# Two token streams that alternate by matmuls in place of weight units, in a four-layer float32 decoder trunk

## The chip, the core and the metric

The kernel runs on one core of one Trainium2 chip. A core has TensorE (matrix products, written into PSUM banks), ScalarE (ACT), VectorE (DVE), GpSimd (POOL) and SyncE (SP), whose queue starts the DMAs here. Each engine works through its own queue in order, and semaphores make one wait for another. The metric is the device time of one execution in microseconds. Three runs of the kernel before took 1221.28, 1221.42 and 1222.72 us; the median is 1221.42.

## What is computed

Four decoder layers over 256 tokens with a model width of 1024, all in float32. Each layer has a token mixer and a SwiGLU feed-forward part, each between two RMS norms. Layers 0 and 3 use differential attention with rotary positions, layer 1 stick-breaking attention, layer 2 sliding-window attention with sinks.

```python
for i in range(DEPTH):                     # 4 layers
    hn = rms_norm(x, norm_gains[i, 0])
    m = mixer(hn)                          # kind i % 3; input projection, attention, w_out
    x = x + rms_norm(m, norm_gains[i, 1])
    f = swiglu(rms_norm(x, norm_gains[i, 2]), ffn_w_gate[i], ffn_w_up[i], ffn_w_down[i])
    x = x + rms_norm(f, norm_gains[i, 3])

def swiglu(h, w_gate, w_up, w_down):       # hidden width 2816
    return (jax.nn.silu(h @ w_gate) * (h @ w_up)) @ w_down
```

(`mixer` stands here for the three attention functions.)

## The kernel before

**Tokens.** The 256 tokens are two streams of 128, stream 0 and stream 1. Both run through the same layers; stream 1 needs keys and values of stream 0.

**Weights.** All weights pass once through the core, cut into 378 units of 128 x 1024 float32 in the order in which a stream needs them. `load_dma` (L240) brings a unit into one of 4 staging buffers, `split` (L252) makes two float32r parts of it, `hi` on ScalarE and `lo` on VectorE, in a ring of 11 slots (L30, L162). A slot is free again when both streams have used its unit. Activations are split in the same way, and a product is the sum of three matmuls: high by hi, high by lo, low by hi.

**Products.** `project` (L494) does one chunk of an input projection, or of gate and up, into one PSUM bank: 4 units with six matmuls of 512 columns each (two blocks of 128 rows: hi, lo, hi, lo with the high part, and then two with the low part). In layer 2 a chunk has 2 units of twelve matmuls of 256 columns. `rows_product` (L468) adds one unit of an output or down projection to two banks, again in six matmuls; the two banks take turns except in the last unit, where one bank is finished before the other (`mm3`, L379). A feed-forward part has 11 chunks of 4 gate-and-up units; the two down units of a chunk follow one chunk later, so that a chunk in the middle costs a stream 6 units. After a chunk come the activation (`t`, `h`) and two transposes (`th`) that give the rows for the down projection.

**Order.** The program is unrolled, and `Emitter` (L41) sets the order in which instructions are emitted. Each stream is a generator that asks for the next unit (`("w",)`), asks to be resumed no earlier than a delay (`("d", ns)`, counted on an estimate of TensorE's time), or waits for an event (`("e", key)`). Attention pieces (transposes, scores, values) run as tasks beside the two streams. `run` (L123) looks at the tasks first in each round, then lets stream 0 go on if it can, otherwise stream 1. Stream 0 may be up to 8 units ahead (`LAG`, L33; `can`, L112). Where stream 1 has yet to pass an edge (the end of an input projection or of a layer) that stream 0 has passed, stream 1 comes first (L139, L140). Since a generator stops only to ask for a unit, a delay or an event, all six matmuls of a unit are emitted together: at full distance the streams alternate unit by unit. A scheduler below the emission assigns the buffers and the waits, and may move an instruction past others that are not ready.

**Small tiles.** Tiles of a few columns (sums, reciprocals, norms: `ss`, `u`, `r`, `nm`, `l`, `half` and others) are in the pool `wk` together with the large working tiles, some constants in `cst`.

All engine calls pass through `Start.run` (L179), so that nearly all rows of the profile name L180; they are told apart by the names of their tiles: `mm_f` gate and up, `acc_f` down, `mm_a`, `mm_b`, `mm_c` the input projections (`mm_a010q` is layer 0, stream 1, group 0, queries), `acc_a`, `acc_b`, `acc_c` the output projections, `th_f` the transposes of the hidden rows, `sc`, `tw`, `ta`, `tpr` and `pv` the attention pieces.

Of the kernel before, what the change touches and what calls it, by code (L numbers as in the profile page):

```python
# [9 lines left out]
F32 = mybir.dt.float32  # L10
# [8 lines left out]
P = 128  # L19
# [21 lines left out]
class Emitter:  # L41
    """Orders the emission of several generators by a running estimate of the tensor engine's time.

    A generator yields ("w",) for the next weight unit, ("d", ns) to be resumed no earlier than ns
    after the tensor engine's work emitted so far, or ("e", key) to wait for an event.
    """

    def __init__(self, load_dma, split, n_units, edges):
        self.t = 0.0
        self.load_dma, self.split, self.n, self.edges = load_dma, split, n_units, edges  # L50
        self.issued = self.loaded = 0
        self.pos = [0, 0]
        self.ring = {}
        self.events = set()
        self.limit = 0
        self.tasks = []
# [101 lines left out]
def trunk_kernel(ctx, tc, x, positions, norm_gains, a_w_in, a_w_out, a_lambda, a_subln, b_w_in, b_w_out,  # L158
# [5 lines left out]
    wk = ctx.enter_context(tc.tile_pool(name="wk", bufs=2))  # L164
    ps = ctx.enter_context(tc.tile_pool(name="ps", bufs=1, space=PSUM))
# [4 lines left out]
    class Start:  # L170
        """An engine whose instructions stay in the order of emission until the start is over."""
# [40 lines left out]
    def downs(c):  # L212
        """The chunks of the down projection that follow chunk c of the gate and up projections."""
# [55 lines left out]
    pos_i = cst.tile([P, 2], I32, name="pos_i")  # L269
# [10 lines left out]
    nsink = cst.tile([P, 16], F32, name="nsink")  # L280
# [4 lines left out]
    inv = cst.tile([P, 32], F32, name="inv")  # L285
    mhalf = cst.tile([P, 8], F32, name="mhalf")
    quarter = cst.tile([P, 1], F32, name="quarter")
    pool.memset(quarter, math.pi / 2)
    act.activation(wk.tile([P, 1], F32, tag="preload", name="preload", bufs=1), quarter, AF.Sin)
# [7 lines left out]
    # additive masks of a block of keys: causal, strictly causal, and the part of the window before the block  # L297
# [12 lines left out]
    gsub = cst.tile([P, 2], F32, name="gsub")  # L310
    lam_init = [0.8 - 0.6 * math.exp(-0.3 * i) for i in (0, 3)]
    nlam = cst.tile([P, 2], F32, name="nlam")
# [3 lines left out]
    def tables():  # L316
        """Generator: cos twice and sin with its sign, per position."""
        magic = 12582912.0
        posf = cst.tile([P, 2], F32, name="posf")
# [28 lines left out]
    def scalars():  # L348
        """-lambda, the negated sinks, and the gains of the inner norm."""
        lsum = wk.tile([P, 4], F32, tag="lsum", name="lsum", bufs=1)  # L350
# [28 lines left out]
    def mm3(o, ah, al, bh, bl, first, last):  # L379
        mm(o, ah, bh, first, False)  # L380
        mm(o, ah, bl, False, False)
        mm(o, al, bh, False, last)

# [4 lines left out]
    def rstd_of(name, s, ss, more=EPS, extra=None):  # L388
        """1/rms from the mean square, or from two parts of it."""
        u = wk.tile([P, 1], F32, tag=f"u{s}", name=f"u_{name}")  # L390
        r = wk.tile([P, 1], F32, tag=f"r{s}", name=f"r_{name}", bufs=3)
# [4 lines left out]
    def first_halves(s, tps, gs, th, tl, name):  # L396
        """The parts of the first layer's input, between the steps of the tables and the first weights."""
# [18 lines left out]
    def pre_norm(s, n, name):  # L416
        """x transposed, times the gain, in two parts; and 1/rms per token."""
        ss = wk.tile([P, 1], F32, tag=f"ss{s}", name=f"ss_{name}")
# [36 lines left out]
    def post_norm(s, acc, gain, name):  # L455
        ss = wk.tile([P, 2], F32, tag=f"ssp{s}", name=f"ssp_{name}")
# [64 lines left out]
    def scaled_tables(s, r, name):  # L521
        """The tables of the keys, and those of the queries, which carry the scores' scale."""
# [24 lines left out]
    def score_products(s, sc, q, k, mask):  # L547
        """The scores of two pairs of heads: the heads of even and of odd number, in half of the array's rows and a bank each."""
# [13 lines left out]
    def split_rows(oT, sl, src, scale=None):  # L562
        """src, times scale, as two float32r parts."""
# [8 lines left out]
    def layer_a(s, i, xn):  # L572
# [20 lines left out]
        def scores(g):  # L593
# [5 lines left out]
            l = st[g] = wk.tile([P, 2, 4], F32, tag=f"l{s}", name=f"l_{name}{g}", bufs=2)  # L599
            el = st[g, "el"] = wk.tile([P, 4], F32, tag=f"el{s}", name=f"el_{name}{g}", bufs=2)  # L600
            ws = {}
            for step in range(3):
                if step < 2:
# [5 lines left out]
                    nm = wk.tile([P, 2, 2], F32, tag=f"nm{s}", name=f"nm_{name}{g}{h0}")  # L609
# [9 lines left out]
                    r = wk.tile([P, 2], F32, tag=f"rl{s}", name=f"rl_{name}{g}{h0}")  # L619
# [19 lines left out]
        def values(g):  # L639
# [8 lines left out]
            ss = wk.tile([P, 4], F32, tag=f"os{s}", name=f"os_{name}{g}")  # L648
# [124 lines left out]
    def layer_c(s, i, xn):  # L773
# [19 lines left out]
        def heads(chunk, g):  # L793
# [17 lines left out]
            nm = wk.tile([P, 2, 2], F32, tag=f"nm{s}", name=f"nm_{name}{g}")  # L811
            es = wk.tile([P, 2, 2], F32, tag=f"es{s}", name=f"es_{name}{g}")
            l = wk.tile([P, 2, 2], F32, tag=f"l{s}", name=f"l_{name}{g}")
# [43 lines left out]
    def ffn(s, i, xn):  # L857
        name = f"f{i}{s}"
        half = wk.tile([P, 1], F32, tag=f"half{s}", name=f"half_{name}", bufs=1)
        hsq = wk.tile([P, 1], F32, tag=f"hsq{s}", name=f"hsq_{name}", bufs=1)  # L860
# [5 lines left out]
        def down(c):  # L866
            nonlocal acc
            for j in range(2):
# [4 lines left out]
                rows_product(acc, hT[c][0][:, j2, :], hT[c][1][:, j2, :], w, c == 0 and j == 0, c == NCH - 1 and j == 1)  # L873
# [78 lines left out]
```

## Time and profile before

| what | value |
|---|---|
| median of 3 runs | 1221.42 us |
| span of the profiled execution | 1220.4 us |
| instructions | 16738 |
| matmuls in the trace | 6028 |
| read from HBM | 203.76 MB, 168 GB/s over the span |
| DMA q1 (all weights) | 54.5% of 16 engines' span |

The profile shows one execution. In a row of groups, the two numbers after the bar are the busy time in all and the mean of one instruction; behind the second bar stands the idle time of the engine ahead of them and what ended it. PE is TensorE's matmuls, PEld its weight loads. In the chain that ended last, a piece has its start, its duration and the number of instructions merged in it, and a piece's duration counts each matmul from its start to the next one's. In the timeline a row has start, duration, engine, operation, output<-inputs and shape; rows that follow each other directly are merged, with their count. A wait's row has the waiting engine and tile, what it waited for, the sum in us, the number of waits and the longest.

### The profile page before, as it was taken

Reading aid. Unit: us, or ns where it says so; the run is one execution under the profiler, and the core shown is the slowest. Engines: PE = TensorE matmul, PEld = TensorE weight load, DVE = VectorE, ACT = ScalarE, POOL = GpSimd, SP = SyncE. Lnnn points to the kernel's source line nnn. Section 1 sums busy time; section 2 is a strip of 40 time slices with the busy share of each in tenths; the row PEclk is TensorE's granted clock in tenths of the full one; section 3 lists DMA queues with packets and bytes.
Section 4 is the critical chain, followed back from the end, with each engine's and each line's share of the span. In section 5 each row is a group of like instructions: output and inputs, shape, how many; then the busy total and the mean of one; then the engine's idle time right before and its main releaser. Section 6 shows DMA issues by size and latency. Waiting matters only on the chain.

```text
span 1220.4 us, 16738 instructions
## 1 busy us (share of the span) xinstructions
PE 1202.2 (99%) x6028; PEld 971.7 (80%) x6028; DVE 779.3 (64%) x1217; ACT 656.7 (54%) x1197; POOL 48.1 (4%) x141
## 2 busy tenths in 40 slices
PE   8999999999999999999999999999999999999997
PEld 6787788888878788888888778888878778888886
DVE  7866665555847666555578666555586776655553
ACT  5665644444756654444477664444474565544442
POOL 2000100000200000000000010000010001000000
PEclk9999999999999999999999999999999999999999
DMA  8635465566743546656564246565565453656550
GB/s 274 205 118 157 155 190 184 179 189 183 219 133 121 173 139 189 190 175 187 184 197 137 87 149 187 183 188 182 182 202 151 131 173 121 181 183 189 179 166 35
DMA packets 140838, 205.90 MB, mean 169 GB/s; under 512 B 9554, under 2 KB 104916, under 8 KB 140756
## 3 DMA queue, kind: packets, MB, share of 16 engines
q1 hardware_dynamic: 140048, 204.51, 54.5%
q8 instruction: 47, 0.77, 0.3%
q10 hardware_dynamic: 708, 0.34, 0.1%
q14 instruction: 35, 0.29, 0.1%
HBM read 203.76 MB, written 1.05 MB: 168 GB/s over the span
## 4 chain that ended last, share of the span: by engine, by line
PE 90%; DVE 4%; ACT 2%; issue 1%; DMA 1%; POOL 1%; DVEq 0%; ACTq 0%; POOLq 0%
PE mm_f L180 39%; PE acc_f L180 18%; PE acc_a L180 3%; PE mm_c L180 2%; PE acc_b L180 2%; DVE lo L180 2%; PE sc_a L180 2%; PE th_f L180 2%; PE acc_c L180 1%; PE sc_b L180 1%; ACT hi L180 1%; DMA stage<-in_a_w_in_dram 1%; PE pv_a L180 1%; PE sc_c L180 1%; DVE x L180 1%
## 5 line engine op out<-in xcount | busy, mean ns | idle before, releaser
L180 DVE TENSOR_TENSOR lo<-stage,hi 128x1024 fp32r<-128x1024 f32 x378 | 460.9, 1223 | 297.7 <-ACT hi L180 295.9
L180 ACT ACTIVATE hi<-stage 128x1024 fp32r<-128x1024 f32 x378 | 399.4, 1061 | 333.8 <-PE mm_f L180 160.0
L180 PE MATMUL mm_f<-hi,xh_q 128*128 128x512 f32 x704 | 283.5, 403 | 0.0
L180 PE MATMUL mm_f<-lo,xh_q 128*128 128x512 f32 x704 | 278.6, 396 | 0.0
L180 PE MATMUL mm_f<-hi,xl_q 128*128 128x512 f32 x704 | 221.0, 395 | 0.9 <-DVE xl_q L180 0.9
L180 PEld LDWEIGHTS mm_f<-hi,xl_q 128*128 128x128 f32 x704 | 132.5, 188 | 34.2 <-DVE xl_q L180 1.8
L180 PEld LDWEIGHTS mm_f<-hi,xh_q 128*128 128x128 f32 x704 | 132.3, 188 | 28.7 <-ACT xh_q L180 0.2
L180 PEld LDWEIGHTS mm_f<-lo,xh_q 128*128 128x128 f32 x704 | 132.4, 188 | 28.4
L180 PE MATMUL acc_f<-hi,hTh_f 128*128 128x512 f32 x352 | 114.9, 402 | 0.5 <-ACT hTh_f L180 0.5
L180 PE MATMUL acc_f<-hi,hTl_f 128*128 128x512 f32 x352 | 111.9, 394 | 0.8 <-DVE hTl_f L180 0.8
L180 PE MATMUL acc_f<-lo,hTh_f 128*128 128x512 f32 x352 | 111.5, 392 | 0.0
L180 ACT ACTIVATE t_f<-mm_f,half_f 128x256 f32<-128x256 f32 x88 | 41.8, 475 | 83.6 <-PE mm_f L180 82.6
L180 PEld LDWEIGHTS acc_f<-hi,hTl_f 128*128 128x128 f32 x352 | 65.9, 188 | 16.0 <-DVE hTl_f L180 1.4
L180 PEld LDWEIGHTS acc_f<-lo,hTh_f 128*128 128x128 f32 x352 | 66.1, 188 | 15.3
L180 PEld LDWEIGHTS acc_f<-hi,hTh_f 128*128 128x128 f32 x352 | 63.8, 188 | 13.4 <-ACT hTh_f L180 0.8
L180 DVE SCALAR_TENSOR_TENSOR t_f<-t_f,mm_f 128x256 f32<-128x256 f32 x88 | 36.7, 417 | 37.5 <-ACT t_f L180 37.4
L180 DVE SCALAR_TENSOR_TENSOR h_f<-t_f,hsq_f,mm_f 128x256 f32<-128x256 f32 x88 | 42.2, 480 | 2.7
L180 ACT ACTIVATE hTh_f<-th_f 128x256 fp32r<-128x256 f32 x88 | 33.0, 376 | 18.1 <-PE th_f L180 17.8
L180 DVE TENSOR_TENSOR hTl_f<-th_f,hTh_f 128x256 fp32r<-128x256 f32 x88 | 36.5, 418 | 5.9 <-ACT hTh_f L180 5.9
L180 ACT ACTIVATE e_a<-sc_a,nm_a 128x128 f32<-128x128 f32 (+1 forms) x64 | 26.0, 421 | 17.0 <-DVE nm_a L180 16.9
L180 PEld LDWEIGHTS th_f<-ident,h_f 128*128 128x128 f32 x176 | 24.4, 140 | 11.5
L180 PE MATMUL th_f<-ident,h_f 128*128 128x128 f32 x176 | 33.5, 272 | 0.0
(584 smaller groups left out, 1545.0 us busy)
## 6 DMA issues: line engine op xcount, KB each, us to landing
stage<-in_ffn_w_gate_dram SPq DMA_DIRECT2D x176, 256.0 KB, 2.8
stage<-in_ffn_w_up_dram SPq DMA_DIRECT2D x176, 256.0 KB, 3.1
stage<-in_ffn_w_down_dram SPq DMA_DIRECT2D x88, 512.0 KB, 3.5
stage<-in_a_w_in_dram SPq DMA_DIRECT2D x48, 512.0 KB, 3.9
stage<-in_b_w_in_dram SPq DMA_DIRECT2D x24, 512.0 KB, 3.8
stage<-in_a_w_out_dram SPq DMA_DIRECT2D x16, 512.0 KB, 3.7
stage<-in_c_w_in_dram SPq DMA_DIRECT2D x10, 512.0 KB, 3.8
gain<-in_norm_gains_dram SPq DMA_DIRECT2D x8, 512.0 KB, 4.1
```

The lines of the kernel that those rows point to most:

```text
L180: i = call(*args, **kw)
```

## The change

The generators of the products stop after each matmul with a new request, `("m",)`, which gives the turn to the other stream. The turn counts only while stream 0 is at least 7 units ahead; there the two streams now alternate matmul by matmul. Elsewhere the order of the streams is as before, but a round, with its look at the tasks and at the ring, now follows each matmul.

```diff
@@ class Emitter
+        self.turn = 0
...
@@ run_main
         elif what[0] == "e":
             m["want"] = what[1]
+        elif what[0] == "m":
+            self.turn = 1 - s
         else:
             m["want"] = "w"
...
@@ run
             behind = any(self.pos[1] < w <= self.pos[0] for w in self.edges)
-            order = mains[::-1] if behind else mains
+            apart = self.pos[0] - self.pos[1] >= LAG - 1
+            order = mains[::-1] if behind or apart and self.turn else mains
...
@@ rows_product
         cols = [slice(h * 512, (h + 1) * 512) for h in range(2)]
+        steps = [(h, a, v) for a, v in ((ah, 0), (ah, 1), (al, 0)) for h in range(2)]
         if last:
-            for h, cs in enumerate(cols):
-                mm3(acc[h], ah, al, w[0][:, cs], w[1][:, cs], first, last)
-        else:
-            for v in range(2):
-                for h, cs in enumerate(cols):
-                    mm(acc[h], ah, w[v][:, cs], first and v == 0, False)
-            for h, cs in enumerate(cols):
-                mm(acc[h], al, w[0][:, cs], False, False)
+            steps.sort(key=lambda step: step[0])
+        for h, a, v in steps:
+            mm(acc[h], a, w[v][:, cols[h]], first and v == 0 and a is ah, last and a is al)
+            yield ("m",)
...
@@ out_proj, and in the same way down in ffn
-            rows_product(acc, oh, ol, w, kt == 0, kt == KT - 1)
+            yield from rows_product(acc, oh, ol, w, kt == 0, kt == KT - 1)
...
@@ project
                 for v in range(2):
                     mm(b, xn[0][:, kt, :], w[v][:, cs], kt == 0 and v == 0, False)
+                    yield ("m",)
             for kt, cs in js:
                 mm(b, xn[1][:, kt, :], w[0][:, cs], False, kt == KT - 1)
+                yield ("m",)
...
@@ trunk_kernel
     wk = ctx.enter_context(tc.tile_pool(name="wk", bufs=2))
+    sm = ctx.enter_context(tc.tile_pool(name="sm", bufs=2))
```

The order of the matmuls within a unit stays. The small tiles, and the small constants of `cst`, are now taken from the pool `sm`, each with the number of buffers that it had, for example:

```diff
-        u = wk.tile([P, 1], F32, tag=f"u{s}", name=f"u_{name}")
+        u = sm.tile([P, 1], F32, tag=f"u{s}", name=f"u_{name}")
...
-    nsink = cst.tile([P, 16], F32, name="nsink")
+    nsink = sm.tile([P, 16], F32, name="nsink", bufs=1)
```

Docstrings and comments are gone, and with them nothing that runs.

More of the change, by code (lines that the diff above doesn't have):

```diff
@@ L267, in trunk_kernel @@
         nc.tensor.matmul(warm, zero, zero, start=True, stop=True)
-    pos_i = cst.tile([P, 2], I32, name="pos_i")
+    pos_i = sm.tile([P, 2], I32, name="pos_i", bufs=1)
     nc.scalar.dma_start(pos_i, positions.rearrange("b (s p) -> p (b s)", p=P))
@@ L283, in trunk_kernel @@
     nc.scalar.dma_start(nsink, c_sinks[0].partition_broadcast(P))
-    inv = cst.tile([P, 32], F32, name="inv")
-    mhalf = cst.tile([P, 8], F32, name="mhalf")
-    quarter = cst.tile([P, 1], F32, name="quarter")
+    inv = sm.tile([P, 32], F32, name="inv", bufs=1)
+    mhalf = sm.tile([P, 8], F32, name="mhalf", bufs=1)
+    quarter = sm.tile([P, 1], F32, name="quarter", bufs=1)
     pool.memset(quarter, math.pi / 2)
-    act.activation(wk.tile([P, 1], F32, tag="preload", name="preload", bufs=1), quarter, AF.Sin)
+    act.activation(sm.tile([P, 1], F32, tag="preload", name="preload", bufs=1), quarter, AF.Sin)
     for j in range(32):
@@ L309, in trunk_kernel @@
     gains = cst.tile([P, P], F32, name="gains")
-    gsub = cst.tile([P, 2], F32, name="gsub")
+    gsub = sm.tile([P, 2], F32, name="gsub", bufs=1)
     lam_init = [0.8 - 0.6 * math.exp(-0.3 * i) for i in (0, 3)]
-    nlam = cst.tile([P, 2], F32, name="nlam")
+    nlam = sm.tile([P, 2], F32, name="nlam", bufs=1)
     cosf = cst.tile([P, 2, 64], F32, name="cosf")
@@ L318, in tables @@
         magic = 12582912.0
-        posf = cst.tile([P, 2], F32, name="posf")
+        posf = sm.tile([P, 2], F32, name="posf", bufs=1)
         r, k, kh, kl, c = (wk.tile([P, 64], F32, tag="t2k", name=f"rt_{n}", bufs=TMP) for n in ("r", "k", "kh", "kl", "c"))
@@ L348, in scalars @@
     def scalars():
-        lsum = wk.tile([P, 4], F32, tag="lsum", name="lsum", bufs=1)
+        lsum = sm.tile([P, 4], F32, tag="lsum", name="lsum", bufs=1)
         lprod = wk.tile([P, 4, 64], F32, tag="t2k", name="lprod", bufs=TMP)
@@ L377, in mm @@
         em.t += n * COLUMN_NS * (4 if f32 else 1)
[L379 to L382, printed above, removed]
     def transpose(o, i):
@@ L416, in pre_norm @@
     def pre_norm(s, n, name):
-        ss = wk.tile([P, 1], F32, tag=f"ss{s}", name=f"ss_{name}")
+        ss = sm.tile([P, 1], F32, tag=f"ss{s}", name=f"ss_{name}")
         th = wk.tile([P, KT, P], F32R, tag=f"xh{s}", name=f"xh_{name}", bufs=1)
@@ L598, in scores @@
             wT[g] = wk.tile([P, 4, nk, P], F32, tag=f"wT{s}", name=f"wT_{name}{g}", bufs=1)
-            l = st[g] = wk.tile([P, 2, 4], F32, tag=f"l{s}", name=f"l_{name}{g}", bufs=2)
-            el = st[g, "el"] = wk.tile([P, 4], F32, tag=f"el{s}", name=f"el_{name}{g}", bufs=2)
+            l = st[g] = sm.tile([P, 2, 4], F32, tag=f"l{s}", name=f"l_{name}{g}", bufs=2)
+            el = st[g, "el"] = sm.tile([P, 4], F32, tag=f"el{s}", name=f"el_{name}{g}", bufs=2)
             ws = {}
@@ L810, in heads @@
             em.set((name, "s", g))
-            nm = wk.tile([P, 2, 2], F32, tag=f"nm{s}", name=f"nm_{name}{g}")
-            es = wk.tile([P, 2, 2], F32, tag=f"es{s}", name=f"es_{name}{g}")
-            l = wk.tile([P, 2, 2], F32, tag=f"l{s}", name=f"l_{name}{g}")
+            nm = sm.tile([P, 2, 2], F32, tag=f"nm{s}", name=f"nm_{name}{g}")
+            es = sm.tile([P, 2, 2], F32, tag=f"es{s}", name=f"es_{name}{g}")
+            l = sm.tile([P, 2, 2], F32, tag=f"l{s}", name=f"l_{name}{g}")
             sink = nsink[:, 4 * g:4 * g + 4].rearrange("p (b j) -> p j b", j=2)
@@ L858, in ffn @@
         name = f"f{i}{s}"
-        half = wk.tile([P, 1], F32, tag=f"half{s}", name=f"half_{name}", bufs=1)
-        hsq = wk.tile([P, 1], F32, tag=f"hsq{s}", name=f"hsq_{name}", bufs=1)
+        half = sm.tile([P, 1], F32, tag=f"half{s}", name=f"half_{name}", bufs=1)
+        hsq = sm.tile([P, 1], F32, tag=f"hsq{s}", name=f"hsq_{name}", bufs=1)
         dve.tensor_scalar(half, xn[2], 0.5, None, ALU.mult)
@@ L872, in down @@
                 j2 = 2 * (c % 2) + j
-                rows_product(acc, hT[c][0][:, j2, :], hT[c][1][:, j2, :], w, c == 0 and j == 0, c == NCH - 1 and j == 1)
+                yield from rows_product(acc, hT[c][0][:, j2, :], hT[c][1][:, j2, :], w, c == 0 and j == 0,
+                                        c == NCH - 1 and j == 1)
             del hT[c]
```

10 lines of the change are left out of this document (5 added, 5 removed).

## The prediction

> **What bounds the kernel now.** I read the page's busy shares first, then the chain that ended last by engine.
>
> ```profile
> PE 1202.2 (99%) x6028; PEld 971.7 (80%) x6028; DVE 779.3 (64%) x1217; ACT 656.7 (54%) x1197; POOL 48.1 (4%) x141
> ...
> PEclk9999999999999999999999999999999999999999
> ...
> PE 90%; DVE 4%; ACT 2%; issue 1%; DMA 1%; POOL 1%; DVEq 0%; ACTq 0%; POOLq 0%
> ```
>
> TensorE is busy for 99% of the span, its clock is granted in full in all 40 slices, and it holds 90% of the chain. The time is therefore the sum of what each matmul takes in the stream plus the few waits. A busy time per matmul overlaps its neighbours, so it can't be used as a price: what counts is the distance from one start to the next. The groups say how many matmuls there are, and the pieces of the chain give the distance.
>
> ```profile
> L180 PE MATMUL mm_f<-hi,xh_q 128*128 128x512 f32 x704 | 283.5, 403 | 0.0
> L180 PE MATMUL mm_f<-lo,xh_q 128*128 128x512 f32 x704 | 278.6, 396 | 0.0
> L180 PE MATMUL mm_f<-hi,xl_q 128*128 128x512 f32 x704 | 221.0, 395 | 0.9 <-DVE xl_q L180 0.9
> L180 PE MATMUL acc_f<-hi,hTh_f 128*128 128x512 f32 x352 | 114.9, 402 | 0.5 <-ACT hTh_f L180 0.5
> ```
>
> ```profile
> 207.39 1.37 PE acc_f L180 x6
> 208.75 0.22 PE th_f L180 x2
> 208.97 8.38 PE mm_f L180 x36
> 217.36 1.37 PE acc_f L180 x6
> 218.73 1.40 PE mm_f L180 x6
> 220.13 1.39 PE acc_f L180 x6
> ...
> 226.11 8.38 PE mm_f L180 x36
> ...
> 325.39 5.62 PE mm_b100q L180 x24
> ...
> 422.63 4.12 PE acc_b L180 x18
> ```
>
> The first two stretches, at 208.97 and 226.11, are 17.1 us apart: this is the steady pattern of the feed-forward part. In 17.1 us each stream does one chunk of 4 gate-and-up units and 2 down units of six matmuls, 72 in all, and the streams alternate by units. Three distances come out:
> - 24 matmuls of one stream in a row (mm_b100q): 5.62 / 24 = 234 ns.
> - 36 matmuls in which the stream changes after every sixth: 8.38 / 36 = 232.8 ns.
> - 18 output matmuls (acc_b): 4.12 / 18 = 228.9 ns.
>
> So the order in which matmuls follow each other does seem to matter by a few ns, and 4000 of them make a few ns worth 10 us.
>
> **The change, part by part.** *Docstrings, comments, pool of small tiles.* The small tiles keep their number of buffers, so no wait comes or goes: 0. Their move shifts addresses of other tiles; the trace shows no case of this, I take 0, and the differences of order below are the nearest rows for what it could do.
>
> *Turns.* No instruction is added and none removed. The product generators now stop after every matmul, and while the first stream is 7 or 8 units ahead the two streams alternate by matmuls. How many does this move? In a feed-forward part a stream has 44 gate-and-up units; the first stream does its first 8 units alone (all gate-and-up), the second its last 8 (2 of them gate-and-up, 6 down). That leaves 36 + 42 = 78 of 88 units, times 6 matmuls and 4 layers: 1872 of the 704 x 3 = 2112. In layers 0, 1 and 3 there are 24 input units per stream, 864 matmuls; their delays keep the streams nearer to each other at times, and I count half, 430. Together 2300. The down and output matmuls already follow each other at 228.9 ns, and I leave them there.
>
> What does a moved matmul cost? It then has a matmul of the other stream on both sides. The trace of before has this just twice, in the first layer:
>
> ```profile
> 22.37 0.39 PE L180 MATMUL mm_a000k<-hi,xh_n 128*128 128x512 f32 x1
> 22.59 0.40 PE L180 MATMUL mm_a010q<-hi,xh_n 128*128 128x512 f32 x1
> ...
> 28.42 0.39 PE L180 MATMUL mm_a010q<-lo,xh_n 128*128 128x512 f32 x1
> 28.65 0.39 PE L180 MATMUL mm_a000k<-lo,xh_n 128*128 128x512 f32 x1
> ```
>
> The matmul at 22.37 (of the first stream, between two of the second) takes 220 ns and that at 28.42 takes 230 ns, to the 10 ns of this view; 225 on the mean. The second way to it: no change of stream gives 234.2 ns, one change in six gives 232.8, so a change is worth (234.2 - 232.8) x 6 = 8 ns, and one after each matmul would give 226. Against it: if it were the change of accumulator that helps, three matmuls in a row into one should be slow, and in the last unit of an output projection they aren't.
>
> ```profile
> 425.23 0.39 PE L180 MATMUL acc_b<-hi,oh_b 128*128 128x512 f32 x1
> ...
> 426.59 0.60 PE L180 MATMUL ta_b<-ident,b_b 128*128 128x128 f32 x4
> ```
>
> Six matmuls, three and three into the two accumulators, take 1.36 us, 226.7 ns each. So I don't know the cause. The bounds are 226 ns (the extrapolation) and 234.2 (the run without any change of stream, as if alternating lost what the changes give now); I take 229, the distance of the acc_b row, which is what a stream of mixed order runs at. The sum: 2300 x (232.8 - 229) = 8.7 us less, with ends of 2300 x 6.8 = 15.6 us less and 2300 x 1.4 = 3.2 us more.
>
> The Trainium skill speaks against this gain: "TensorE: Matmul & The Clock Gate", section "Back-to-back issue gap", makes the isolated distance of warm matmuls depend on the columns alone, 512 / 2.4 + 2.5, about 216 ns. The trace does not agree in size (232.8) nor in being one number (228.9 to 234), but by this rule the change's sum would be 0 from the order of matmuls.
>
> *What hides the steady part's other work.* ScalarE and VectorE between a chunk's end and its transposes:
>
> ```profile
> 214.60 1.06 ACT L180 ACTIVATE hi<-stage 128x1024 fp32r<-128x1024 f32 x1 [1.74 <-PE mm_f L180]
> 216.00 0.47 ACT L180 ACTIVATE t_f<-mm_f,half_f 128x256 f32<-128x256 f32 x1 [0.33 <-PE mm_f L180]
> ...
> 215.70 1.23 DVE L180 TENSOR_TENSOR lo<-stage,hi 128x1024 fp32r<-128x1024 f32 x1 [1.57 <-ACT hi L180]
> ...
> 217.29 0.48 DVE L180 SCALAR_TENSOR_TENSOR h_f<-t_f,hsq_f,mm_f 128x256 f32<-128x256 f32 x1
> ...
> 221.35 0.38 PE L180 MATMUL th_f<-ident,h_f 128*128 128x128 f32 x2
> ```
>
> The hidden row is done at 217.77 and its transposes start at 221.35: 3.6 us of cover. With turns the transposes still stand two units of each stream behind the chunk's end, so the cover stays. The ring is tighter. A slot comes free when the second stream has finished its unit; ScalarE's hi waits for just this (1.74 us idle at 214.60), and hi and lo are done 2.3 us after its start (1.23 us from 215.70). Before, the first stream needs the unit in that slot six units of 1.4 us after the release, 8.4 us; with turns both streams finish together and two pairs stand between, 5.6 us. That covers the 2.3 us. The DMAs behind it are moved by no more than this. In the steady part nothing else is late.
>
> *Tasks.* Attention pieces are looked at after every matmul rather than after every unit, also where the streams don't take turns. A piece whose delay has run out comes half a unit, 0.7 us, earlier on the mean, so its inputs have less time. What already waits:
>
> ```profile
> ACT hi L180 <- PE mm_f L180: 160.0, 121, 1.7
> ...
> PEld pv_c L180 <- ACT pT_c L180: 1.9, 4, 0.9
> PEld sc_a L180 <- ACT e_a L180: 1.8, 5, 0.6
> PEld sc_a L180 <- ACT kT_a L180: 1.5, 3, 0.8
> ...
> PEld tpr_c L180 <- ACT pT_c L180: 1.1, 4, 0.4
> ...
> PEld ta_b L180 <- ACT aT_b L180: 0.9, 3, 0.4
> ```
>
> These five have 19 waits. Nothing to 19 x 0.7 = 13 us is possible; many have slack or are set by the other engine's queue, and I take 1.5 us. Below nothing is possible too: a wait can be filled by the other stream's matmuls; the five rows sum to 7.2 us, the most that could go.
>
> *Sum.* 1220.4 (the span) - 8.7 + 1.5 = 1213.2. The median of the runs, 1221.42, is 1.0 us above the profiled span, so I predict 1214.2 us.
>
> **The rivals.**
> *No gain from the order.* The distance is set by the columns and the weights, and differences between stretches are chance patterns of each stretch. For it: the row at 425.23, where one order gives 226.7, and the fact that each matmul loads its weights anew (as many PEld as PE) before and after. Then only the tasks' 1.5 us are left: 1222.9, within 0.2% of before (2.4 us, about what a measurement of this kernel can tell from no change). The rule cited above gives the same.
> *The turns don't come about.* If the scheduler below the emission puts the units back together, or if the streams are rarely 7 apart, fewer matmuls move. Against it: the regular 17.1 us pattern has the two streams alternating by units, as they do at a distance of 7 to 8. It gives 1221.4.
> *Slower: ScalarE's queue is held up in the attention layers.* The second stream's unit is spread over 12 matmuls in place of 6, and its ring slot comes free 6 x 0.233 = 1.4 us later after its start. The hi of the next unit stands in ScalarE's queue until then, and exp and copies stand behind it. For it: ScalarE sat idle at hi for 160 us behind mm_f alone. In the steady part 3.6 us of cover swallow it; in attention the 19 waits above have no cover. If 12 of them grow by 1.4 us, it costs 16.8 us, and with the gain of 8.7 the time is 1229.5. It decides from 9 waits on (1221.4 - 8.7 + 12.6 = 1225.3); with no gain from the order, from 2.
>
> **How the numbers follow.** Forecast 0.57; no gain 0.16; no turns 0.06; slower 0.21. The forecast's own ends are 1221.4 - 15.6 = 1205.8 and about 1219. For 8 in 10 I drop the fastest tenth and the upper half of the slower rival: 1207.5 to 1225.5. Faster by over 0.2% holds the forecast, 0.57; within 0.2% the two rivals without effect, 0.22; slower 0.21.
>
> **What would show it.** In the steady part two mm_f matmuls of one unit stand 0.46 us apart with one of the other stream between, the pattern of 17.1 us shrinks to 17.1 - 48 x 0.0038 = 16.9 us, and 36 matmuls of a stretch take 8.24 in place of 8.38 us. If the pattern stays at 17.1, the order has no price and the first rival holds. If it shrinks while the total doesn't, the difference stands in the attention parts as PEld waits for e_a, kT_a, pT_c and aT_b, longer than the 7.2 us above, with ScalarE's hi waits ahead of them. I am wrong if distances grow above 234 ns, or if the ring makes TensorE wait for hi or lo in the feed-forward part.

## The result, and the profile after

| kernel | median, us | runs | ratio to before | span of the profiled execution, us |
|---|---|---|---|---|
| before | 1222.07 | 1221.28 to 1223.63 | 1 | 1220.4 |
| after | 1240.77 | 1240.37 to 1242.32 | 1.0158 [1.0143, 1.0172] | 1238.6 |

The change makes the kernel 1.6% slower. 1214.2 was forecast; the time lies above the whole range.

The page of the kernel after begins with nearly the same picture as before: TensorE is busy for the same time (1201.6 us; 1202.2 before), in a span that is 18.2 us longer. The chain that ended last (its shares by engine) seems to say more.

```profile
PE 1201.6 (97%) x6028; PEld 975.4 (79%) x6028; DVE 774.7 (63%) x1217; ACT 651.7 (53%) x1197; POOL 48.4 (4%) x141
...
PE 73%; issue 16%; ACT 4%; DVE 3%; DMA 3%; POOL 1%; SPq 0%; ACTq 0%; DVEq 0%; POOLq 0%
```

TensorE's share of the chain was 90% and is 73%, but that is not time that TensorE lost. Most of the 16% of "issue" is one piece, in which the chain follows GpSimd from one norm to the next (`r_q` to `u_e`); TensorE is busy for 170.43 of its 171.18 us.

```profile
747.76 171.18 issue
```

So the question is first whether the steady part got slower, and then what stands outside it. The first has a quick answer. Of the chain in the kernel after (start, duration, engine and tile, instructions merged), these two pieces start one steady pattern of the feed-forward part each:

```profile
196.54 5.68 PE mm_f L187 x25
...
213.36 5.70 PE mm_f L187 x25
```

They are 16.82 us apart; before it was 17.14. The prediction's sign for its gain (16.9) is there, and its sign for the turns as well: in the same chain the two streams' matmuls alternate, and those of one stream are 0.45 us apart.

```profile
202.23 0.23 PE acc_f L187
202.46 0.23 PE mm_f L187
202.68 0.23 PE acc_f L187
202.91 0.23 PE mm_f L187
203.14 0.23 PE acc_f L187
```

What lies outside is seen where a layer ends. The timeline of before, at the end of layer 0 (a row has start, duration, engine, line, operation, output<-inputs, shapes, count, and in brackets the idle time ahead):

```profile
313.08 0.39 PE L180 MATMUL acc_f<-hi,hTl_f 128*128 128x512 f32 x1
313.31 0.39 PE L180 MATMUL mm_f<-hi,xh_q 128*128 128x512 f32 x1
...
321.58 1.04 PE L180 MATMUL tp_n<-ident,x 128*128 128x128 f32 x8
322.37 0.72 PE L180 MATMUL acc_f<-hi,hTh_f 128*128 128x512 f32 x2
...
325.00 0.39 PE L180 MATMUL acc_f<-hi,hTl_f 128*128 128x512 f32 x1
325.22 0.39 PE L180 MATMUL mm_b100q<-hi,xh_n 128*128 128x512 f32 x1
```

Stream 0 is done with the layer at 313.31. Stream 1 has 8 units left, and under them the norms of stream 0 run: its next transposes (`tp_n`, 321.58) and its next layer (`mm_b100q`, 325.22) follow without a wait. The same place after the change:

```profile
311.66 0.39 PE L187 MATMUL mm_f<-hi,xh_q 128*128 128x512 f32 x1
311.89 0.39 PE L187 MATMUL acc_f<-hi,hTh_f 128*128 128x512 f32 x1
312.12 0.39 PE L187 MATMUL mm_f<-lo,xh_q 128*128 128x512 f32 x1
312.35 0.39 PE L187 MATMUL mm_f<-hi,xh_q 128*128 128x512 f32 x1
...
325.43 0.40 PE L187 MATMUL acc_f<-hi,hTh_f 128*128 128x512 f32 x1
325.67 0.40 PE L187 MATMUL acc_f<-hi,hTl_f 128*128 128x512 f32 x1
...
326.83 0.39 PE L187 MATMUL acc_f<-hi,hTl_f 128*128 128x512 f32 x1
329.60 1.60 PE L187 MATMUL tp_n<-ident,x 128*128 128x128 f32 x8 [2.38 <-DVE x L187]
```

At 311.89 stream 0 does one matmul of its last unit and stops. `pos` counts a unit when it is taken, so with this unit stream 0 counts as past the edge, `behind` is true, and stream 1 comes first. It finishes the unit that it had begun and does its 8 remaining ones. Four of stream 0's five missing matmuls get in at 321.55 to 322.33, while stream 1 waits for its last hidden rows, and the fifth comes at 325.67; stream 1 ends at 326.83. Both end the layer together, nothing of the other is left to cover the norm, and TensorE waits 2.38 us for stream 0's `x`. So it does not hold that the order of the streams is as before wherever they don't take turns, as the section on the change has it. The sums of the waits (waiting engine and tile, what it waited for, us, number, longest) have this place on top, and a number of waits in attention that grew:

```profile
PEld tp_n L187 <- DVE x L187: 9.2, 6, 2.9
PEld mm_f L187 <- ACT xh_q L187: 4.4, 4, 1.2
...
PEld sc_a L187 <- ACT kT_a L187: 3.5, 8, 1.1
PEld pv_a L187 <- ACT wT_a L187: 2.8, 3, 1.3
...
PEld sc_a L187 <- ACT e_a L187: 2.4, 4, 0.8
...
PEld ta_b L187 <- ACT aT_b L187: 1.9, 8, 0.4
```

The waits for `kT_a`, `e_a` and `aT_b` were 1.5, 1.8 and 0.9 us, the one for `xh_q` 0.2; of the first row there was nothing. So three things had to be told apart: where the shorter pattern comes from, what the layer ends cost, and what makes the attention parts longer.

### The profile page after: what moved, and what is told of

Read it like the earlier page. It is cut to its first block, busy times and chain, and to the rows that moved or that the text cites. A ratio compares the mean times of both kernels' runs of the same rounds, so it can differ in the third digit from the quotient of the medians.

```text
span 1238.6 us, 16821 instructions
## 1 busy us (share of the span) xinstructions
PE 1201.6 (97%) x6028; PEld 975.4 (79%) x6028; DVE 774.7 (63%) x1217; ACT 651.7 (53%) x1197; POOL 48.4 (4%) x141
## 4 chain that ended last, share of the span: by engine, by line
PE 73%; issue 16%; ACT 4%; DVE 3%; DMA 3%; POOL 1%; SPq 0%; ACTq 0%; DVEq 0%; POOLq 0%
PE mm_f L187 29%; PE acc_f L187 13%; PE acc_a L187 3%; PE mm_c L187 2%; PE sc_a L187 2%; PE acc_c L187 2%; ACT hi L187 1%; PE acc_b L187 1%; PE th_f L187 1%; DVE lo L187 1%; PE pv_a L187 1%; DVE x L187 1%; DMA stage<-in_a_w_in_dram 1%; DMA gain<-in_norm_gains_dram 1%; PE sc_b L187 1%
## 5 line engine op out<-in xcount | busy, mean ns | idle before, releaser
L187 PE MATMUL mm_f<-hi,xh_q 128*128 128x512 f32 x704 | 257.9, 401 | 2.8 <-ACT xh_q L187 2.8
L187 PE MATMUL mm_f<-lo,xh_q 128*128 128x512 f32 x704 | 250.6, 391 | 0.0
L187 PE MATMUL mm_f<-hi,xl_q 128*128 128x512 f32 x704 | 229.7, 390 | 0.6 <-DVE xl_q L187 0.6
L187 PEld LDWEIGHTS mm_f<-hi,xh_q 128*128 128x128 f32 x704 | 129.8, 188 | 28.3 <-ACT xh_q L187 4.4
L187 PE MATMUL acc_f<-lo,hTh_f 128*128 128x512 f32 x352 | 133.4, 392 | 0.0
L187 PE MATMUL acc_f<-hi,hTh_f 128*128 128x512 f32 x352 | 131.3, 391 | 2.1 <-ACT hTh_f L187 2.1
L187 PE MATMUL acc_f<-hi,hTl_f 128*128 128x512 f32 x352 | 132.2, 390 | 0.4
```

Source lines behind the costliest of these rows:

```text
L187: i = call(*args, **kw)
```

## The experiments

All times are medians of the runs of one kernel; the runs of before beside them had medians of 1221.1 to 1221.9 us. Three of the kernels need a word on addresses: offsets are the tiles' start addresses within a partition, in bytes, as the built programs assign them.

### Each part of the change alone

**The pool without the turns.** The kernel after, without the stops after each matmul:

```diff
         for h, a, v in steps:
             mm(acc[h], a, w[v][:, cols[h]], ...)
-            yield ("m",)
```

(and the same twice in `project`).

> The small tiles in their own pool, the streams in the order of before. Theory (addresses): the shorter distance of the gate-and-up matmuls comes from where the pool puts the large tiles, so it is here too: about 227 to 228 ns in place of 233, the waits as before, 1203 to 1208 us. Rival (turns): the distance falls because the streams alternate, so it is 233 ns here and the time 1220 to 1224 us.

Measured: 1205.31 us (1204.93 to 1205.52), ratio 0.9868 [0.9853, 0.9883]. The edit that the prediction priced at nothing is worth 15.8 us, and this kernel beats both.

**The turns without the pool.** The kernel before with the stops, `turn` and `apart`, and all tiles in their old pools.

> The turns, the small tiles in the pools of before. Theory (addresses): distance 233 ns as before, and the whole loss of the turns shows, about 35 us: 1252 to 1260 us. Rival (turns shorten the distance): 228 ns and 1238 to 1243 us.

Measured: 1252.84 us (1252.04 to 1253.35), ratio 1.0259 [1.0242, 1.0276]. The turns alone cost 31.7 us over the 1221.1 of before. The steady pattern in the chains of these two kernels, first the pool alone, then the turns alone:

```profile
206.60 8.19 PE mm_f L187 x36
...
223.43 8.19 PE mm_f L187 x36
```

```profile
215.41 5.80 PE mm_f L184 x25
...
232.51 5.80 PE mm_f L184 x25
```

16.83 us with units emitted whole, 17.10 us with matmuls taking turns: the pattern depends on the pool, and the order of the matmuls changes it by 0.01 (16.83 against 16.82 after) to 0.04 us (17.14 against 17.10).

### Which addresses matter

In the kernel before, the transposed inputs (`xh`, `xl`) start at 96 (stream 0) and 64 (stream 1) modulo 256 bytes, because tiles of 32 bytes stand ahead of them; the hidden rows, the output rows and the ring of weights start at 0. After, all of these start at 128. Two readings were open: that multiples of 128 are fast, or that the stationary and the moving tile of a matmul must have the same offset.

**Only the transposed inputs, at multiples of 128.** The kernel before with dummy tiles:

```diff
+        if n == 0:
+            nc.gpsimd.memset(wk.tile([P, (8, 16)[s]], F32, tag=f"pada{s}", ...), 0.0)
         th = wk.tile([P, KT, P], F32R, tag=f"xh{s}", ...)
         tl = wk.tile([P, KT, P], F32R, tag=f"xl{s}", ...)
+        if n == 0:
+            nc.gpsimd.memset(wk.tile([P, (24, 16)[s]], F32, tag=f"padb{s}", ...), 0.0)
```

> The kernel before with its order and its pools, and with four small dummy tiles that only push the transposed inputs (high and low part, both streams) to multiples of 128 bytes in the partition (they began at 96 and 64 modulo 128). It adds four short memsets on GpSimd at the start. Alignment theory (the start address of the operand that TensorE loads as weights sets the distance of matmuls): 1205 us (1203 to 1209), distance of 512-column gate-and-up matmuls about 228 ns as in the kernel with the pool alone. Rival (the gain of the pool comes from something else that moves with it, such as the small tiles' own addresses, the constants, or which tiles stand beside each other): 1219 to 1223 us and 232 to 234 ns.

Measured: 1216.16 us (1215.61 to 1216.35), ratio 0.9955 [0.994, 0.997]. A third of the gain: neither theory. The trace says why. The dummies also moved the hidden and output rows: stream 0's stationary tiles now stand at 128 modulo 256, stream 1's at 0, the ring at 0. Where stream 1 runs alone, at a layer's end, its gate-and-up matmuls are 226.7 ns apart and its down matmuls too; where the streams alternate, units of stream 1 with some 228 ns from matmul to matmul and units of stream 0 with some 233 ns take turns. Stream 0 starts at a multiple of 128 and is slow. That leaves the difference between the two operands modulo 256.

**Only the ring, by 128 bytes.** The pool alone, with one dummy tile of 32 columns ahead of the ring and one of 96 behind it. All large tiles are still at multiples of 128.

> The kernel with the pool alone (1205.3 us, order of before), with dummy tiles that push only the ring of weights by 128 bytes and put the tiles behind it back: every large tile still starts at a multiple of 128 bytes, the stationary tiles at 128 modulo 256, the ring now at 0 modulo 256 (it was at 128). Congruence theory (a 512-column matmul takes 226.7 ns when its stationary tile and its moving tile start at the same offset modulo 256 bytes, and about 231 to 233 otherwise, whatever the offset is): both gate-and-up and down matmuls are slow, 231 to 233 ns, and the time is 1219 to 1227 us. Alignment theory (starts at multiples of 128 bytes are what counts): 227 to 228 ns and 1204 to 1208 us.

Measured: 1222.54 us (1221.71 to 1224.61), ratio 1.0009 [1.0, 1.0019]: the whole gain is gone.

**All stationary tiles congruent with the ring.** The kernel before with its pools, as two experiments above, with dummies of (40, 48) and (24, 16) columns.

> The kernel before with its order and its pools and with four dummy tiles that push the stationary tiles of both streams: transposed inputs to 256 modulo 512 bytes, hidden and output rows to 0 modulo 512, the ring stays at 0 modulo 512. Most small tiles, constants and the second stream's working tiles stay at uneven offsets. Congruence modulo 256: all 512-column matmuls settle at 226.7 ns, 1203 to 1208 us. Congruence modulo 512: the gate-and-up and input matmuls stay at 231 to 233 ns and only the down and output matmuls are fast, 1216 to 1221 us. If the small tiles or constants matter in another way: over 1210 us with no clear pattern.

Measured: 1207.52 us (1206.69 to 1208.69), ratio 0.9886 [0.9871, 0.99], although the small tiles are still in the pool of the large ones. That is 14.0 us of gain by addresses alone; the 2.2 us to the pool alone are not explained. The chains, first of the shifted ring, then of the padded kernel:

```profile
208.43 8.37 PE mm_f L187 x36
...
225.59 8.37 PE mm_f L187 x36
```

```profile
207.28 8.21 PE mm_f L180 x36
...
224.12 8.21 PE mm_f L180 x36
```

17.16 us where ring and stationary tiles differ by 128 bytes, 16.84 us where they agree modulo 256 (in the padded kernel the inputs differ from the ring by 256 of 512, so 512 isn't the period). Five sets of addresses follow the one rule.

### What the layer ends cost

**The edge rule mended.** The kernel after, where stream 1 comes first only once stream 0 has finished the unit it began:

```diff
+        if s == 0:
+            self.open = what[0] == "m"
...
-            behind = any(self.pos[1] < w <= self.pos[0] for w in self.edges)
+            behind = any(self.pos[1] < w <= self.pos[0] for w in self.edges) and not self.open
```

> As the changed kernel, but the second stream goes first behind an edge only once the first has finished the unit that it has begun. Theory (edge): the loss is that the first stream's last unit ahead of an edge lies unfinished for eight units of the second, so it goes away here: 1203 to 1209 us, no wait of tp_n for x over 0.5 us. Rival (finer turns and earlier tasks cost the waits all over the attention layers): the loss stays, 1230 to 1241 us.

Measured: 1228.03 us (1227.36 to 1228.41), ratio 1.0054 [1.0039, 1.0069]. The waits of `tp_n` for `x` went from 9.2 to 0.4 us, as expected, but the edge is worth 12.7 us, not the 35.5 us between after and the pool alone. 22.7 us remain, and the theory that the edge explains the whole loss fell. By the pages of this kernel and of the pool alone, TensorE is idle for 13.1 us more (31.8 against 18.7) and busy for 9.2 us more (1194.2 against 1185.0).

**No alternation.** The kernel after with `apart = False`: it stops after each matmul, but stream 0 always goes on first.

> As the changed kernel, the generators stop after each matmul, but the streams never take turns at full distance. Theory (edge): the first stream's last unit is still left unfinished, so the loss stays: 1232 to 1244 us, waits of tp_n for x of about 2.5 us. Rival (the alternation itself costs): 1203 to 1212 us.

Measured: 1248.38 us (1246.82 to 1250.88), ratio 1.0223 [1.0208, 1.0238]: 7.6 us slower than after, and above both expected ranges; the waits of `tp_n` for `x` are 1.7 us at most. So the loss doesn't need the alternation. Units are cut open all the same: stream 0 can go on as soon as stream 1 has taken a unit, and in this kernel's trace matmuls of stream 0 stand inside 258 of the units that stream 1 begins at full distance (4 in the pool alone).

### Where the rest is

To see where it arises, take the time at which TensorE has done the same amount of product work (projections, gate and up, down, by their columns) in each trace, less that of the pool alone. It is taken at two places of each feed-forward part of the pool alone: where stream 1 is nine units into it, and at stream 0's last matmul in it. The table has the growth of this lag in us. The last column is what grows between the two places, where both streams are in the feed-forward part; a layer's column is what grows from the second place of the layer before to the first of this one, so that it holds the attention and the hand-overs on both sides of it (layer 0's begins with the span).

| kernel | layer 0 | layer 1 | layer 2 | layer 3 | inside the four feed-forward parts |
|---|---|---|---|---|---|
| after | 5.4 | 10.0 | 9.0 | 9.6 | 0.3 |
| edge mended | 6.0 | 6.6 | 4.5 | 5.0 | 0.2 |
| edge mended, turns in feed-forward only | -0.4 | 0.4 | -0.8 | -1.2 | 0.3 |
| edge mended, turns in projections only | 8.2 | 4.7 | 11.6 | 6.0 | -0.6 |
| edge mended, whole units near each other | 0.1 | 0.9 | 0.2 | 2.0 | 0.3 |

Inside the feed-forward parts nothing is lost, though most of the turns take place there: 2564 of the 3165 changes of stream between one product matmul and the next in the kernel after. Their ends are another matter: counted from its first to its last matmul of either stream, the four parts hold 16.5 us of the lag of after and 3.9 with the edge mended.

**Turns in the feed-forward parts only**, and **in the projections only** (both with the edge mended; `if name[0] == "f"`, or its opposite, ahead of the stops).

> As the kernel after with the edge rule mended, but the products stop after each matmul only in the feed-forward parts; the input and output projections emit whole units. If the 22.7 us that are left arise in the attention parts: 1205 to 1210 us. If they arise in the feed-forward parts (ring, hand-over at their start and end): 1225 to 1229. If by their share of TensorE's time (feed-forward is about 70 percent of the matmuls): about 1221.

> As the kernel after with the edge rule mended, but the products stop after each matmul only in the input and output projections; the feed-forward parts emit whole units. It is the complement of the kernel with turns in the feed-forward parts alone (1203.6 us). Attention theory (all of the 22.7 us left over the pool alone come from the projections' stops): 1226 to 1231 us. Rival (the loss needs stops on both sides of the hand-over between attention and feed-forward): under 1218 us.

Measured: 1203.63 us (1203.36 to 1203.86), ratio 0.9853 [0.9838, 0.9867], the lowest median of all kernels here, though it can't be told from the pool alone; and 1236.99 us (1235.66 to 1238.24), ratio 1.0129 [1.0112, 1.0146]. So the loss comes with the stops in the projections: without them there is none. The second time is 6 us above the expected range and 9 us above that of the kernel with stops in both; which hand-over causes this is open (layer 2's column has the most of it).

**Whole units near each other.** With the edge mended, a stream stops inside a unit only while stream 0 is at least 7 units ahead:

```diff
             what = m["gen"].send(value)
+            while what[0] == "m" and self.pos[0] - self.pos[1] < LAG - 1:
+                what = m["gen"].send(None)
```

> As the kernel after with the edge rule mended, but a stream stops after a matmul only while stream 0 is at least 7 units ahead; nearer than that units are emitted whole, as before. The alternation at full distance is untouched. Interruption theory (units cut open where the streams do not alternate, with pieces and the other stream pushed in between): 1206 to 1212 us. Rival (the alternation at full distance costs it): 1224 to 1230 us.

Measured: 1208.96 us (1208.52 to 1209.35), ratio 0.9895 [0.9879, 0.9912]. This takes back 19.1 of the 22.7 us. But the alternation at full distance was not left untouched. Outside the feed-forward parts (at least one of the two matmuls is of a projection) the stream changes 195 times between one product matmul and the next; with the edge mended it was 703 times, in the pool alone 155. With this limit the streams hardly come to alternate in the projections at all. So the run doesn't tell units that are cut open near each other from turns in the projections. In the waits of this kernel, the waits for the attention inputs are near the size of before, and the one for `wT_a` is down from 2.8 to 0.3 us:

```profile
PEld sc_a L192 <- ACT kT_a L192: 2.2, 5, 0.9
...
PEld sc_a L192 <- ACT e_a L192: 1.1, 3, 0.4
PEld ta_b L192 <- ACT aT_b L192: 1.0, 4, 0.3
...
PEld pv_a L192 <- ACT wT_a L192: 0.3, 1, 0.3
```

**Pieces, or the other stream?** A whole unit keeps two things out: attention pieces, and the other stream. Four kernels, all with the edge mended, were to tell them apart. Attention pieces not looked at while stream 0 is inside a unit (`for task in [] if self.open else list(self.tasks)`):

> As the kernel after with the edge rule mended (1228.0 us), but attention pieces are looked at only when stream 0 is not in the middle of a unit, in place of after every matmul. Tasks theory (the remaining 22.7 us over the pool alone come from pieces that are emitted earlier than their inputs allow): 1206 to 1214 us, with the waits of TensorE for kT_a, wT_a, e_a, aT_b and pT_c back near those of before. Rival, the interleaved order of the streams itself (units held open, both streams reaching their delays and ring slots together): 1225 to 1230 us.

The stream that began a unit goes on with it while they are near, pieces still after each matmul (`order = sorted(mains, key=lambda m: m["s"] != self.begun)`):

> As the kernel after with the edge rule mended (1228.0 us), but while stream 0 is less than 7 units ahead the stream that has begun a unit goes on with it; attention pieces are still looked at after each matmul. If the other stream's cutting in is what costs: 1209 to 1212 us, as with whole units (1209.0). If the pieces in the middle of a unit cost: 1224 to 1229 us. Half and half: about 1218.

The reverse: no pieces inside a unit while they are near, the other stream may cut in:

> As the kernel after with the edge rule mended (1228.0 us), but while stream 0 is less than 7 units ahead no attention piece is looked at in the middle of a unit; the other stream may still cut in after each matmul. If the pieces cost: 1209 to 1212 us. If the other stream's cutting in costs: 1224 to 1229 us. Half and half: about 1218.

Whole units near each other, and pieces held back inside stream 0's units at full distance:

> As the kernel with whole units near each other (1209.0 us), and at full distance too attention pieces are looked at only when stream 0 is not inside a unit. If the 3.7 us that this kernel still loses to the pool alone come from pieces at full distance: 1204 to 1206 us. If from the alternation itself: 1208 to 1211 us.

Measured, in the same order, and beside them the kernels that they are compared with. The last two columns are counted in TensorE's order of matmuls, by the stream and unit of each in the built programs: how often the stream changes with a projection, as above, and how many of the 756 units (378 in each stream) have an attention piece between their first and last matmul. (In the pool alone, too, some do, by the scheduler below the emission.)

| kernel | median, us (runs) | ratio to before | changes | units with a piece inside |
|---|---|---|---|---|
| no pieces inside units of stream 0 | 1220.21 (1218.34 to 1221.01) | 0.9985 [0.9976, 0.9995] | 735 | 80 |
| the stream stays with its unit | 1219.89 (1218.87 to 1221.65) | 0.9985 [0.9976, 0.9995] | 185 | 94 |
| no pieces inside a unit, near | 1228.04 (1227.93 to 1228.8) | 1.005 [1.0035, 1.0065] | 647 | 108 |
| whole units near, pieces held back | 1208.43 (1207.48 to 1209.45) | 0.9891 [0.9875, 0.9908] | 207 | 31 |
| edge mended | 1228.03 | 1.0054 | 703 | 116 |
| whole units near each other | 1208.96 | 0.9895 | 195 | 60 |
| edge mended, turns in feed-forward only | 1203.63 | 0.9853 | 165 | 34 |
| pool alone | 1205.31 | 0.9868 | 155 | 32 |

The first kernel lies between its two ranges. The third one changed little of what it was to change: its flag remembers only whether the stream that emitted last stands inside a unit, so that a piece still gets into an open unit of stream 1 when stream 0 has cut into it and stands between two of its own. With 108 units against 116, its time says little about pieces. The other rows say more. With the other stream kept out (second kernel) 8.1 us are gained. With the pieces kept out as well (whole units) another 10.9 are gained, at about the same number of changes. Fewer pieces inside units at about the same number of changes as with the edge mended (first kernel) gain 7.8. From 60 units to 31 nothing is gained that these runs can tell (1208.4 against 1209.0), so a unit with a piece in it has no fixed price. What is shown is that the stops in the projections are the cause (the kernel with turns in feed-forward only has no loss), and that pieces inside units have a large part in it; shares for pieces, cut-ins and turns that would add up can't be given.

**Turns in the feed-forward parts only, with whole units near each other:**

> The kernel with turns in the feed-forward parts alone (edge rule mended, 1203.6 us), with units emitted whole wherever stream 0 is less than 7 units ahead. If cut units near the ends of a feed-forward part still cost: 1201 to 1203 us. If not: 1203 to 1206 us, as the kernel with the pool alone (1205.3).

Measured: 1204.23 us (1203.79 to 1204.53), ratio 0.9858 [0.9843, 0.9872], as without the addition. In the feed-forward parts cut units cost nothing that these runs can tell.

## Why the prediction was wrong

The gain that was forecast came, and more of it, from the part that was priced at nothing; the loss that turned the sign came from the tasks, priced at 1.5 us, and from the edge rule, which has no term. The 35.5 us between after and the pool alone, undone in this order, and the 15.8 us of the pool:

| what | us |
|---|---|
| pool (14.0 of it by offsets alone, in the padded kernel) | -15.8 |
| edge rule with a begun unit | +12.7 |
| units whole below a distance of 7 (cut units and nearly all turns in the projections) | +19.1 |
| the rest, not resolved | +3.7 |
| sum | +19.7 |

Measured against the 1221.1 us of before that ran beside the pool alone: 1240.77 - 1221.12 = 19.7, which it must be, as each term is a difference of two of these kernels. In another order the terms would have other sizes.

- **What bounds the kernel** was right: TensorE, and the distance from one matmul to the next.
- **Pool of small tiles: 0.** This step failed first. It looked for waits and found none, named the shift of addresses, and dropped it as without a case in the trace. The cases were there: the three distances that the prediction read as an effect of order. Down and output matmuls, whose stationary tiles agreed with the ring, settle at 226.7 ns where several of their units follow each other; gate-and-up and `mm_b100q`, at 96 and 64 modulo 256, stay at 233 to 234; the `acc_b` stretch, at 228.9, settles only from its seventh matmul on. "So I don't know the cause" was the place to ask what else differs between the two groups, and the operand is the first thing that does.
- **Turns: 8.7 us less.** The steady pattern shrank by even more than was forecast (17.14 to 16.82 us, forecast 16.9), but by another cause, so that this sign came true by luck. (The sum's upper end, 3.2 us more, would also have given a forecast's end of 1224.6; the "about 1219" isn't worked out.) As far as the turns go, the rival without gain from the order held: with units whole, in the pool alone, the pattern is 16.83 us and 36 matmuls take 8.19; with turns the pattern is 16.82. The rule that the prediction cited from the Trainium skill, "TensorE: Matmul & The Clock Gate", section "Back-to-back issue gap", makes the distance of isolated warm matmuls depend on the columns alone. The traces agree in that the order has nearly no price; they don't agree with a single number, as 226.7 and about 233 ns both occur for the same columns, by the operands' offsets.
- **What hides the steady part's other work** was right: inside the four feed-forward parts the kernel after lost 0.3 us.
- **Tasks: 1.5 us more.** This step failed by its size and by what it looked at. It priced only pieces that come half a unit early, by the waits that were there before. These five rows grew no more than from 7.2 to 9.8 us in the kernel after. It missed that pieces now stand inside units and that every stop is also a place where the other stream may cut in: together with the turns in the projections 19.1 us, of which 10.9 go with the pieces when the other stream is already kept out. Its bound of 13 was too low.
- **The edge rule** isn't in the prediction at all. It read that stream 1 comes first past an edge, and that a stream now stops inside a unit, but not that `pos` counts the unit when it is taken: 12.7 us.
- **The slower rival** had the right sign, but no run speaks for its mechanism. It blamed stream 1's unit spread over twelve matmuls in the attention layers, and ScalarE's wait for the slot. The wait for gate-and-up matmuls did grow, from 160.0 us before:

```profile
ACT hi L187 <- PE mm_f L187: 226.2, 153, 2.2
```

But with turns in the feed-forward parts only it is nearly as long, and that kernel loses nothing to the pool alone:

```profile
ACT hi L190 <- PE mm_f L190: 216.2, 146, 2.2
```

The waits of `hi` for matmuls of the projections, where the rival has its cost, are 63.8 us in sum before and 58.7 after.

## What to carry to other kernels

An edit that moves no instruction can still move addresses: where two groups of matmuls of one shape keep different distances, compare the offsets of their operands before looking at their order, and lay out the small tiles so that they shift no large one. A generator that gets new stopping points changes every rule that is asked at a stop: go through each (edges, priorities, pieces) with a half-done unit in mind, and limit the stops to the place for which they are meant. Cover at a layer's end consists of one stream being behind the other; an order that brings both to the end together takes it away.

## What the runs showed of the hardware

**Offsets modulo 256 bytes.** In a row of 512-column float32r matmuls, each with fresh weights, the distance from one start to the next settles at 226.7 ns when the stationary and the moving tile start at the same offset modulo 256 bytes (the pool alone and the padded kernel), and at about 230 to 234 ns when they don't: on the mean 232.5 with a difference of 128 bytes (the shifted ring), 233.1 with 64 and 96 (the kernel before). After transposes it takes some six matmuls (an output projection of the kernel before) to ten (the feed-forward parts of the pool alone) until the shorter distance sets in. Single units that agree, between units that don't, may not reach it: stream 0's down matmuls in the kernel before are 231 ns apart on the median. Over the kernel the offsets are worth 14.0 to 15.8 us, 1.1 to 1.3%. Why they matter wasn't shown.

**The clock after one wait.** TensorE's four longest waits in the kernel after are all about 2.4 us long (2.38 to 2.44) and end at 57.98, 329.60, 642.23 and 921.24 us. Around the end of the first, second and last of them the granted clock fell. Three stretches of the kernel after (stretch, length, busy times of the engines, then PEclk, DMA share and GB/s):

```profile
57.00:60.80 3.80, 2.82 (x7) 2.16 (x8) 3.32 (x6) 0.00 (x0) 0.00 (x0) 0.56 0.47 169
330.50:333.90 3.40, 3.40 (x14) 2.91 (x13) 3.40 (x9) 3.10 (x11) 0.74 (x3) 0.50 0.67 243
921.00:924.40 3.40, 3.16 (x12) 2.87 (x13) 3.40 (x7) 2.75 (x12) 0.86 (x2) 0.50 0.65 226
```

After the wait that ends at 329.60, 3.4 us ran at half clock; by an estimate from this, half of it, 1.7 us, comes on top of the wait of 2.4. Behind the wait of the same length that ends at 642.23 the clock stayed full. In the kernel with the turns alone, waits of 2.39 us end at 332.64, 647.97 and 930.24 us, and the clock fell behind the second alone. What decides isn't shown here.
